# Values on half-width column tiles, shared key tiles and an earlier key projection in an attention mixer

## The chip, the cores and the metric

One core of a Trainium2 chip runs the whole program. The metric is device microseconds of that core, from the first to the last instruction of one launch; three runs of the kernel before are given, and one profiled run.

## What is computed

The program is a chain of blocks over 256 tokens of width 1024, in fp32: a gMLP mixer, a feed-forward part with a convolution, a differential attention, a second such feed-forward part, then a SwiGLU part, a mixer with two kinds of attention, another SwiGLU part and a last norm. The change touches only the mixer with two kinds of attention. In the reference it is (cut):

```python
u = rms_norm(x, mix_norm) @ w_in
c_q, c_kv, k_rope, mq, mk, mv = split(u)              # 384, 256, 32, 512, 512, 512 columns
q = rope_part(rms_norm(c_q, q_norm) @ w_uq)           # 8 heads of 64 + 32
k_nope, v = split(rms_norm(c_kv, kv_norm) @ w_ukv)    # 8 heads of 64 and 64
a_out = causal_softmax(q @ [k_nope, rope(k_rope)].T * 96 ** -0.5) @ v
b_out = causal_softmax(mq @ mk.T * 64 ** -0.5 - slope * distance) @ mv   # 8 heads of 64
x = x + concat(a_out, b_out) @ w_out
```

With 256 tokens the block-sparse attention (MoBA) has one block, its own, so it is dense and causal.

## The kernel before, in words

Weights come as 351 units of 128 x 1024 in fp32. A unit is loaded by SyncE (`Weights.load`, L296 on), its high part is copied by ScalarE (`prep_hi`, L305) and its low part is subtracted by VectorE (`prep_lo`, L311), and TensorE multiplies with both, so that three products in the fast fp32 format stand for one of full precision. `feed()` prepares a unit if fewer than `ahead` (6) prepared units are unused; a preparation also asks for loads up to `LOADS` (4) units on. Unit, high part and low part each take a place in one pool of 36 slots of 128 x 1024 (`slot`), and so do nearly all other large tiles: scores, their transposes, biases, values, compressed keys. A slot is handed to a new tile when the last reader of the tile before it is through; the engine that writes the new tile first waits for that reader.

The mixer stage runs from some 755 to 880 us. It works on pairs of heads: 16 heads are 8 pairs, which the table calls 0 to 7 (0 to 3 the first kind, 4 to 7 MoBA; q alone counts single heads). A pair has the two heads on the halves of the 128 partitions. The order of TensorE, ScalarE and VectorE is written out by hand in two tables, `MIX_BEFORE` (a scheduler may still move what is in it) and `MIX_PAIRS` (kept as written); each entry is a letter with its number:

- S: scores into PSUM on TensorE (L1148 for 0 to 3, all 128 rows of the array; L1152 for 4 to 7, two products of 64 rows side by side). N: `biased`, scale, bias and maximum on VectorE into the SBUF tile `s` (L846). E: exponentials on ScalarE (L1168). M: `normed`, division by the sum on VectorE (L1172, L1175).
- T: transposes of the probabilities on TensorE (L1182) and their copy on ScalarE (L1183). V: `values`, probabilities times values on TensorE (L1190). H and L: high and low part of the result (L1202, L1206). o: output projection (`part`, L535). b: the bias tile `al` (L1140).
- k: `mla_keys`, the rope-free keys `pkn` (L351 to L353; 4 column chunks). v: `mla_values` (L419). q: `mla_project`, queries of one head into `qs` (matmul `pqn`, copy L1129, VectorE L1130). p: `moba_project`, `mqk` of a pair of heads (matmul `pq` L375 to L378, ScalarE L390, VectorE L397).
- F, wh, wl: `feed`, high and low part of a weight unit; mid: loads the next gain.

Before S(4) the numbered steps 0 to 3 hold the projections q and p; from step 3 on a step is S(c), T(c−1), N(c), V(c−2), E, wl, M, H, L and then fillers.

The values stand in zero-padded tiles: for each half of the heads and each block of 128 tokens (tb) one tile of 128 x 4 x 2 x 128, in which the value columns of the first head of a pair are in the first 64 of 128 columns, and those of the second head in the last 64; GpSimd clears the rest (L1034), `put_values` (L1039) copies the other 64 columns with ScalarE. V then has 4 matmuls, all into the same 128 partitions of `po`, which add up. The compressed keys (`ckv`) are two tiles, high and low.

Where the mixer ends, a junction adds the result (L484), norms (L456, L445, L451, L501), transposes the tokens (L509) and splits them into `x` (L512 on ScalarE, L519 on VectorE); the last feed-forward part begins with token-major products `pz` (L419) on the units that are ready.

Of the kernel before, what the change touches and what calls it, by code (L numbers as in the profile page):

```python
# [11 lines left out]
F32R = mybir.dt.float32r  # L12
BF16 = mybir.dt.bfloat16
I32 = mybir.dt.int32
AF = mybir.ActivationFunctionType
# [5 lines left out]
P = 128  # L21
T = 256
# [9 lines left out]
AHEAD = 6  # L32
LOADS = 4
# [22 lines left out]
S, N_, E, M, T_, V, H_, L_, B_ = [(lambda c, x=x: (x, c, 0)) for x in "SNEMTVHLb"]  # L56
F, wh, wl, mid_ = ("F", 0, 0), ("wh", 0, 0), ("wl", 0, 0), ("mid", 0, 0)
k, v, q = (lambda c: ("k", c, 0)), (lambda tb: ("v", tb, 0)), (lambda h: ("q", h, 0))
p, o = (lambda c, n: ("p", c, n)), (lambda tb, c: ("o", tb, c))
MIX_BEFORE = [k(0), F, k(1), F, k(2), F, v(0), F, v(1), F, q(0), q(1), wh]  # L60


def _step(c, *fill):

    return [S(c), T_(c - 1), N_(c), V(c - 2), E(c), wl, M(c), H_(c - 2), L_(c - 2), *fill]


MIX_PAIRS = [
    S(0), N_(0), E(0), wl, q(2), M(0), wh, q(3), p(0, 1),
    S(1), T_(0), N_(1), E(1), wl, M(1), q(4), q(5), wh, k(3), p(1, 1),  # L70
    S(2), T_(1), N_(2), E(2), wl, M(2), q(6), q(7), V(0), H_(0), L_(0), wh,
    *_step(3, wh, p(2, 0), wl, B_(4), wh, o(0, 0)),
    *_step(4, mid_, wh, p(2, 1), wl, B_(5), wh, o(0, 1)),
    *_step(5, wh, p(3, 0), wl, B_(6), wh, o(0, 2)),
    *_step(6, wh, wl, B_(7), p(3, 1), wh),
    *_step(7, wh, o(0, 3), wl, wh, o(0, 4)), o(1, 0), wl, o(1, 1),
    T_(7), V(6), F, H_(6), L_(6), o(0, 5), V(7), H_(7), L_(7), o(0, 6), F, o(0, 7),
]
MIX = MIX_BEFORE + MIX_PAIRS

# [155 lines left out]
def _build(ctx, tc, nc, a, out):  # L236
# [10 lines left out]
    mm, act, vec = nc.tensor.matmul, nc.scalar.activation, nc.vector  # L247
# [3 lines left out]
    def nm(s):  # L251
        uid[0] += 1
        return f"{s}_{uid[0]}"

    def slot(name, dt=F32, shape=(P, D)):
        return slotp.tile(list(shape), dt, name=nm(name), tag="slot")
# [4 lines left out]
    def col(name, shape=(P, 1), dt=F32, bufs=4):  # L261
        return small.tile(list(shape), dt, name=nm(name), tag=name, bufs=bufs)

    def psm(name):
        return psM.tile([P, 512], F32, name=nm(name), tag="mm")
# [5 lines left out]
    def wide(tb, name):  # L271

        return [psA.tile([P, 512], F32, name=nm(name), tag=f"acc{tb}{q}") for q in range(2)]
# [13 lines left out]
    class Weights:  # L287
        def __init__(self):
            self.loaded, self.prepped, self.used, self.hi = [], [], 0, None
            self.ahead = AHEAD  # L290

        def load(self, n, cols=(slice(0, D),)):
            while len(self.loaded) < min(n, N_UNITS):
# [5 lines left out]

        def prep_hi(self, cols=(slice(0, D),)):  # L300
            n = len(self.prepped)
            self.load(n + LOADS)
            self.hi = slot(f"wh{n}", F32R)
            for c in cols:
                act(self.hi[:, c], self.loaded[n][:, c], AF.Copy)  # L305
# [37 lines left out]
    W = Weights()  # L343
    feed, unit = W.feed, W.unit
# [14 lines left out]
    def block(x, tb, n=KD):  # L359

        return [(x[:, k, 0, TB[tb]], x[:, k, 1, TB[tb]]) for k in range(n)]

    def pairs(x, tb, n):

        return [(x[0][:, tb, k, :], x[1][:, tb, k, :]) for k in range(n)]
# [661 lines left out]
    def mixer(x, late, tables, mid):  # L1027
        CS, dist, mask, kr, pair = tables
        cg = held["cg"]

        vals = [[slot("vals", shape=(P, 4, 2, P)) for tb in range(2)] for n in range(2)]
        for t in vals[0] + vals[1]:
            for n in range(2):
                nc.gpsimd.memset(t[:, :, n, (1 - n) * 64:(2 - n) * 64], 0.0)  # L1034

        def put_values(t, ps):
            ps = ps.rearrange("p (c n d) -> p c n d", c=4, n=2)
            for n in range(2):
                act(t[:, :, n, n * 64:(n + 1) * 64], ps[:, :, n, :], AF.Copy)  # L1039


        cq = [slot("cq", F32R, (P, 2, 3, P)) for n in range(2)]
        ckv = [slot("ckv", F32R, (P, 2, 2, P)) for n in range(2)]
        w1, w2 = W.lazy(8), W.lazy(2)
        stage = []

        def groups(tb):
            pa = wide(tb, "pmix")
            pk = psm("pckv")
            ops = token_major([(pa[0], 0, 512), (pa[1][:, :416], 512, 928)], block(x, tb), w1, D)  # L1050
            ops += token_major([(pk[:, :T], 0, T)], block(x, tb), w2, T)

            def done():
                cn = slot("cn", shape=(P, 768))

                kr_, two = pa[1][:, 384:416], cn[:, 640:768].rearrange("p (r s d) -> p r s d", r=2, s=2)
                for s_, d, n, o in ((0, 0, 32, 0), (1, 0, 16, 16), (1, 16, 16, 0)):
                    vec.tensor_copy(two[:, :, s_, d:d + n], kr_[:, o:o + n].unsqueeze(1).to_broadcast([P, 2, n]))
                for ps, n, o in ((pa[1][:, :384], 384, 0), (pk[:, :T], 256, 384)):
                    ms = col("cms")  # L1060
                    act(cn[:, o:o + n], ps, AF.Square, accum_out=ms)
                    r = rsqrt_col(ms, mul=1.0 / n)
                    vec.scalar_tensor_tensor(out=cn[:, o:o + n], in0=ps, scalar=r, in1=cg[:, o:o + n], op0=ALU.mult, op1=ALU.mult)
                put_values(vals[1][tb], pa[0])
                stage.append(cn)
            return ops, done
        start(x, late, groups)
# [47 lines left out]
        def mla_values(tb):  # L1115
            pvv = psm("pv")
            for f, _ in token_major([(pvv, 0, 512)], pairs(ckv, tb, 2), lambda i: kv(1), 512):
                f()
            put_values(vals[0][tb], pvv)

        wq = W.lazy(3)

# [62 lines left out]
        def values(g):  # L1185

            po, aT = psm("po")[:, :T], HH[g]["aT"]
            for n in range(2):
                for tb in range(2):
                    mm(out=po[:, tb * P:T], lhsT=vals[g // 4][tb][:, g % 4, n, :], rhs=aT[:, n, tb * T:tb * T + T - tb * P], start=(n + tb == 0), stop=(n + tb == 2))  # L1190
            HH[g] = {"po": po, "hid": hid_tiles()}

        hids, ws = [], {}
# [10 lines left out]
        def low(g):  # L1204
            hid = HH[g]["hid"]
            vec.tensor_sub(hid[1], HH[g]["po"], hid[0].bitcast(F32))  # L1206
            hids.append(hid)

        do = {
            "S": scores, "N": biased, "E": exps, "M": normed, "T": attend, "V": values, "H": high, "L": low, "b": bias,  # L1210
            "k": mla_keys, "v": mla_values, "q": mla_project, "p": moba_project, "o": project_out,
            "F": feed, "wh": W.prep_hi, "wl": W.prep_lo, "mid": mid,
        }

        def run(todo):

            for kind, i, c in todo:
                do[kind](*((i, c) if kind in ("p", "o") else () if kind in ("F", "wh", "wl", "mid") else (i,)))

        run(MIX_BEFORE)  # L1220
        with tc.manual_schedule(engines={mybir.EngineType.PE, mybir.EngineType.Activation, mybir.EngineType.DVE}):
            run(MIX_PAIRS)
        n = proj.count[1]
        assert proj.count[0] == 8 and all(o(1, c) in MIX for c in range(n))
        proj.held = [(hids[c], ws[c]) for c in range(n, 8)]
# [160 lines left out]
    for n, (c0, c1) in enumerate(ranges):  # L1386
        c, sum_ = slice(c0, c1), n < 2
# [16 lines left out]
    for c0, c1 in ranges[1:]:  # L1404
        c = slice(c0, c1)
# [47 lines left out]
```

## Time and profile before

| | |
|---|---|
| three runs | 1073.36, 1075.0, 1074.91 us, median 1074.91 |
| profiled execution | 1075.8 us, span of the trace 1074.0 |
| mean granted clock of TensorE | 0.996 |
| TensorE busy | 1054.1 us, 98% of the span |
| VectorE, ScalarE, GpSimd busy | 776.6, 656.7, 34.8 us |
| read from memory | 194.94 MB |

The table is from the first lines of the profile page. Busy time counts an engine's instructions from start to end; matmuls overlap, so what a group of matmuls costs is best read from the start of its first to the start of what follows it. Times in the trace are counted from the start of the span. An idle time in brackets names the instruction that ended it.

### The profile page before, as it was taken

Reading aid. Unit: us, or ns where it says so; the run is one execution under the profiler, and the core shown is the slowest. Engines: PE = TensorE matmul, PEld = TensorE weight load, DVE = VectorE, ACT = ScalarE, POOL = GpSimd, SP = SyncE. Lnnn points to the kernel's source line nnn. Section 1 sums busy time; section 2 is a strip of 40 time slices with the busy share of each in tenths; the row PEclk is TensorE's granted clock in tenths of the full one; section 3 lists DMA queues with packets and bytes.
Section 4 is the critical chain, followed back from the end, with each engine's and each line's share of the span. In section 5 each row is a group of like instructions: output and inputs, shape, how many; then the busy total and the mean of one; then the engine's idle time right before and its main releaser. Section 6 shows DMA issues by size and latency. Waiting matters only on the chain. (4 is left out here: it accounts for less than half of the span.)

```text
span 1074.0 us, 15781 instructions
## 1 busy us (share of the span) xinstructions
PE 1054.1 (98%) x5802; PEld 901.1 (84%) x5802; DVE 776.6 (72%) x1360; ACT 656.7 (61%) x1226; POOL 34.8 (3%) x65
## 2 busy tenths in 40 slices
PE   8999999999999999999999999999998999999997
PEld 6988888888787788888888888888897788888886
DVE  5896989887668768998776796665576857956633
ACT  5655867765478758776654675554476647755522
POOL 0100000000000110000000010000100000000000
PEclk9999999999999999999999999999999999999999
DMA  9946548652555456676525666553443455765501
GB/s 339 342 155 235 177 164 309 200 182 92 201 175 174 138 178 201 215 249 197 181 101 186 212 215 223 189 188 114 147 148 140 140 173 198 243 207 194 178 2 39
DMA packets 57246, 197.04 MB, mean 183 GB/s; under 512 B 6952, under 2 KB 9040, under 8 KB 57168
## 3 DMA queue, kind: packets, MB, share of 16 engines
q1 hardware_dynamic: 57024, 195.77, 54.4%
q8 instruction: 45, 0.74, 0.3%
q14 instruction: 33, 0.27, 0.1%
q10 hardware_dynamic: 144, 0.26, 0.1%
HBM read 194.94 MB, written 1.06 MB: 182 GB/s over the span
## 5 line engine op out<-in xcount | busy, mean ns | idle before, releaser
L311 DVE TENSOR_TENSOR wl<-w,wh 128x1024 fp32r<-128x1024 f32 (+1 forms) x352 | 424.8, 1219 | 130.8 <-ACT wh L305 91.2
L376 PE MATMUL pu<-x,wh 128*128 128x512 f32 x1216 | 427.2, 396 | 0.0
L305 ACT ACTIVATE wh<-w 128x1024 fp32r<-128x1024 f32 (+1 forms) x352 | 363.0, 1051 | 98.0 <-DVE wl L311 63.2
L375 PE MATMUL pu<-x,wl 128*128 128x256 f32 x1064 | 296.7, 279 | 0.0
L376 PEld LDWEIGHTS pu<-x,wh 128*128 128x128 f32 x1216 | 222.7, 188 | 44.6 <-DVE y L673 0.6
L375 PEld LDWEIGHTS pu<-x,wl 128*128 128x128 f32 x1064 | 200.6, 189 | 6.6
L535 PE MATMUL acc<-wh,hh 128*128 128x512 f32 x434 | 146.2, 397 | 1.3 <-DVE o L929 0.9
L535 PE MATMUL acc<-wl,hh 128*128 128x512 f32 x434 | 143.1, 390 | 0.0
L535 PE MATMUL acc<-wh,hl 128*128 128x512 f32 x434 | 142.1, 390 | 0.0
L390 ACT ACTIVATE low<-pu 128x256 f32<-128x256 f32 x152 | 57.4, 377 | 76.5 <-PE pu L376 75.8
L535 PEld LDWEIGHTS acc<-wh,hl 128*128 128x128 f32 x434 | 81.5, 188 | 17.5 <-DVE hl L429 0.3
L535 PEld LDWEIGHTS acc<-wl,hh 128*128 128x128 f32 x434 | 81.4, 188 | 16.9
L535 PEld LDWEIGHTS acc<-wh,hh 128*128 128x128 f32 x434 | 80.2, 188 | 15.5 <-ACT hh L428 1.4
L376 PE MATMUL pq<-x,wh 128*128 128x512 f32 x192 | 70.7, 405 | 0.0
L397 DVE TENSOR_TENSOR low<-pu,low 128x256 f32<-128x256 f32 x114 | 47.7, 418 | 17.3 <-ACT low L390 17.3
L419 PE MATMUL pz<-wh,x 128*128 128x256 f32 (+1 forms) x288 | 58.2, 323 | 0.8 <-DVE x L519 0.8
L428 ACT ACTIVATE hh<-y 128x256 fp32r<-128x256 f32 x88 | 35.6, 409 | 29.2 <-DVE y L673 15.1
L661 ACT ACTIVATE y<-low,cw 128x256 f32<-128x256 f32 x76 | 45.0, 592 | 11.7 <-DVE low L397 11.4
L419 PEld LDWEIGHTS pz<-wh,x 128*128 128x128 f32 x288 | 43.1, 189 | 6.5 <-DVE x L519 2.1
L375 PE MATMUL pq<-x,wl 128*128 128x256 f32 x168 | 47.6, 284 | 0.0
L456 ACT ACTIVATE junk<-h 128x512 bf16<-128x512 f32 (+1 forms) x32 | 19.9, 622 | 40.1 <-DVE h L484 19.1
L429 DVE TENSOR_TENSOR hl<-y,hh 128x256 fp32r<-128x256 f32 x88 | 36.6, 420 | 9.9 <-ACT hh L428 9.8
(235 smaller groups left out, 1257.0 us busy)
## 6 DMA issues: line engine op xcount, KB each, us to landing
w<-in_wall SPq DMA_DIRECT2D x349, 512.0 KB, 4.1
gain<-in_norm_g SPq DMA_DIRECT2D x7, 512.0 KB, 7.7
h<-in_x SPq DMA_DIRECT2D x4, 256.0 KB, 5.9
w<-in_wall SPq DMA_DIRECT2D x4, 256.0 KB, 5.2
bias<-fd SPq DMA_DIRECT2D x2, 512.0 KB, 10.2
gain<-in_ffn_norm SPq DMA_DIRECT2D x2, 512.0 KB, 4.8
gain<-in_a_ln_g SPq DMA_DIRECT2D x1, 512.0 KB, 6.3
gain<-in_a_ln_b SPq DMA_DIRECT2D x1, 512.0 KB, 6.6
```

The lines of the kernel that those rows point to most:

```text
L305: act(self.hi[:, c], self.loaded[n][:, c], AF.Copy)
L311: vec.tensor_sub(wl[:, c], w[:, c], wh[:, c].bitcast(F32))
L375: mm(out=ps[:, T:], lhsT=wl, rhs=x[:, k, 0], start=False, stop=False)
L376: mm(out=ps, lhsT=wh, rhs=x[:, k], start=(k == 0), stop=(k == KD - 1))
L390: act(low, ps[:, T:], AF.Copy)
L397: vec.tensor_add(out_, hi, low)
L419: mm(out=d, lhsT=x[lr], rhs=ws(u)[hl][:, c], start=(k == 0 and lr == 0 and hl == 0), stop=(k == last and lr == 1))
L428: act(hi, src, AF.Copy)
L429: vec.tensor_sub(lo, src, hi.bitcast(F32))
L456: act(junk[:, :src.shape[-1]], src, AF.Square, scale=1.0 / 32.0, accum_out=ms)
L535: mm(out=self.acc[tb][q], lhsT=hid[x][:, TB[tb]], rhs=w[hl][:, HALF[q]], start=s, stop=e)
L661: act(y, ps, AF.Identity, scale=cw[:, f, 2:3], bias=cw[:, f, 3:4])
```

## The change

- The values have two tiles without padding, of 128 x 2 x 512 (one for each half of the heads, both token blocks in it). The memsets are gone, and `put_values` is one copy of 128 x 512. V has 4 matmuls of 64 columns of weights: the two heads of a pair write partitions 0 to 63 and 64 to 127 of `po`, each with a sum of its own.
- The compressed keys, high and low, share one tile.
- k(3) moves from behind q(5) in step 1 into `MIX_BEFORE`; in step 0, q(3) goes ahead of a `wh`.
- In the mixer `loads` is 3 and `ahead` is 4; from `mid` on `ahead` is 6 again. One F of `MIX_BEFORE` is gone, and one pair of wh and wl of step 6.
- In step 7, T(6) and V(5) come ahead of S(7).

```diff
@@ -57,7 +57,7 @@
 F, wh, wl, mid_ = ("F", 0, 0), ("wh", 0, 0), ("wl", 0, 0), ("mid", 0, 0)
 k, v, q = (lambda c: ("k", c, 0)), (lambda tb: ("v", tb, 0)), (lambda h: ("q", h, 0))
 p, o = (lambda c, n: ("p", c, n)), (lambda tb, c: ("o", tb, c))
-MIX_BEFORE = [k(0), F, k(1), F, k(2), F, v(0), F, v(1), F, q(0), q(1), wh]
+MIX_BEFORE = [k(0), F, k(1), F, k(2), k(3), F, v(0), v(1), F, q(0), q(1), wh]
 
 
 def _step(c, *fill):
@@ -66,14 +66,14 @@
 
 
 MIX_PAIRS = [
-    S(0), N_(0), E(0), wl, q(2), M(0), wh, q(3), p(0, 1),
-    S(1), T_(0), N_(1), E(1), wl, M(1), q(4), q(5), wh, k(3), p(1, 1),
+    S(0), N_(0), E(0), wl, q(2), M(0), q(3), wh, p(0, 1),
+    S(1), T_(0), N_(1), E(1), wl, M(1), q(4), q(5), wh, p(1, 1),
     S(2), T_(1), N_(2), E(2), wl, M(2), q(6), q(7), V(0), H_(0), L_(0), wh,
     *_step(3, wh, p(2, 0), wl, B_(4), wh, o(0, 0)),
     *_step(4, mid_, wh, p(2, 1), wl, B_(5), wh, o(0, 1)),
     *_step(5, wh, p(3, 0), wl, B_(6), wh, o(0, 2)),
-    *_step(6, wh, wl, B_(7), p(3, 1), wh),
-    *_step(7, wh, o(0, 3), wl, wh, o(0, 4)), o(1, 0), wl, o(1, 1),
+    *_step(6, B_(7), p(3, 1), wh),
+    T_(6), V(5), S(7), N_(7), E(7), wl, M(7), H_(5), L_(5), wh, o(0, 3), wl, wh, o(0, 4), o(1, 0), wl, o(1, 1),
     T_(7), V(6), F, H_(6), L_(6), o(0, 5), V(7), H_(7), L_(7), o(0, 6), F, o(0, 7),
 ]
 MIX = MIX_BEFORE + MIX_PAIRS
@@ -287,7 +287,7 @@
     class Weights:
         def __init__(self):
             self.loaded, self.prepped, self.used, self.hi = [], [], 0, None
-            self.ahead = AHEAD
+            self.ahead, self.loads = AHEAD, LOADS
 
         def load(self, n, cols=(slice(0, D),)):
             while len(self.loaded) < min(n, N_UNITS):
@@ -299,7 +299,7 @@
 
         def prep_hi(self, cols=(slice(0, D),)):
             n = len(self.prepped)
-            self.load(n + LOADS)
+            self.load(n + self.loads)
             self.hi = slot(f"wh{n}", F32R)
             for c in cols:
                 act(self.hi[:, c], self.loaded[n][:, c], AF.Copy)
@@ -1028,19 +1028,12 @@
         CS, dist, mask, kr, pair = tables
         cg = held["cg"]
 
-        vals = [[slot("vals", shape=(P, 4, 2, P)) for tb in range(2)] for n in range(2)]
-        for t in vals[0] + vals[1]:
-            for n in range(2):
-                nc.gpsimd.memset(t[:, :, n, (1 - n) * 64:(2 - n) * 64], 0.0)
-
-        def put_values(t, ps):
-            ps = ps.rearrange("p (c n d) -> p c n d", c=4, n=2)
-            for n in range(2):
-                act(t[:, :, n, n * 64:(n + 1) * 64], ps[:, :, n, :], AF.Copy)
+        vals = [slot("vals", shape=(P, 2, 512)) for n in range(2)]
 
 
         cq = [slot("cq", F32R, (P, 2, 3, P)) for n in range(2)]
-        ckv = [slot("ckv", F32R, (P, 2, 2, P)) for n in range(2)]
+        kvt = slot("ckv", F32R, (P, 2, 2, 2, P))
+        ckv = [kvt[:, n] for n in range(2)]
         w1, w2 = W.lazy(8), W.lazy(2)
         stage = []
 
@@ -1061,7 +1054,7 @@
                     act(cn[:, o:o + n], ps, AF.Square, accum_out=ms)
                     r = rsqrt_col(ms, mul=1.0 / n)
                     vec.scalar_tensor_tensor(out=cn[:, o:o + n], in0=ps, scalar=r, in1=cg[:, o:o + n], op0=ALU.mult, op1=ALU.mult)
-                put_values(vals[1][tb], pa[0])
+                act(vals[1][:, tb, :], pa[0], AF.Copy)
                 stage.append(cn)
             return ops, done
         start(x, late, groups)
@@ -1116,7 +1109,7 @@
             pvv = psm("pv")
             for f, _ in token_major([(pvv, 0, 512)], pairs(ckv, tb, 2), lambda i: kv(1), 512):
                 f()
-            put_values(vals[0][tb], pvv)
+            act(vals[0][:, tb, :], pvv, AF.Copy)
 
         wq = W.lazy(3)
 
@@ -1185,9 +1178,10 @@
         def values(g):
 
             po, aT = psm("po")[:, :T], HH[g]["aT"]
-            for n in range(2):
-                for tb in range(2):
-                    mm(out=po[:, tb * P:T], lhsT=vals[g // 4][tb][:, g % 4, n, :], rhs=aT[:, n, tb * T:tb * T + T - tb * P], start=(n + tb == 0), stop=(n + tb == 2))
+            for tb in range(2):
+                for n in range(2):
+                    d = (2 * (g % 4) + n) * 64
+                    mm(out=po[n * 64:(n + 1) * 64, tb * P:T], lhsT=vals[g // 4][:, tb, d:d + 64], rhs=aT[:, n, tb * T:tb * T + T - tb * P], start=(tb == 0), stop=(tb == 1))
             HH[g] = {"po": po, "hid": hid_tiles()}
 
         hids, ws = [], {}
@@ -1206,10 +1200,14 @@
             vec.tensor_sub(hid[1], HH[g]["po"], hid[0].bitcast(F32))
             hids.append(hid)
 
+        def half_way():
+            W.ahead = AHEAD
+            mid()
+
         do = {
             "S": scores, "N": biased, "E": exps, "M": normed, "T": attend, "V": values, "H": high, "L": low, "b": bias,
             "k": mla_keys, "v": mla_values, "q": mla_project, "p": moba_project, "o": project_out,
-            "F": feed, "wh": W.prep_hi, "wl": W.prep_lo, "mid": mid,
+            "F": feed, "wh": W.prep_hi, "wl": W.prep_lo, "mid": half_way,
         }
 
         def run(todo):
@@ -1217,9 +1215,11 @@
             for kind, i, c in todo:
                 do[kind](*((i, c) if kind in ("p", "o") else () if kind in ("F", "wh", "wl", "mid") else (i,)))
 
+        W.loads, W.ahead = 3, 4
         run(MIX_BEFORE)
         with tc.manual_schedule(engines={mybir.EngineType.PE, mybir.EngineType.Activation, mybir.EngineType.DVE}):
             run(MIX_PAIRS)
+        W.loads, W.ahead = LOADS, AHEAD
         n = proj.count[1]
         assert proj.count[0] == 8 and all(o(1, c) in MIX for c in range(n))
         proj.held = [(hids[c], ws[c]) for c in range(n, 8)]
```

Three places in the order of instructions. First, TensorE in step 1 (`pkn` is k(3), `pqn` is q(5), `pq` is p(1, 1)); before:

```order
L353 MATMUL pqn_8554<-cq_7980,wl_1816_8292 128x256
L351 MATMUL pkn_8570<-ckv_7982,wh_1775_8079 128x256
L352 MATMUL pkn_8570<-ckv_7983,wh_1775_8079 128x256
L353 MATMUL pkn_8570<-ckv_7982,wl_1776_8081 128x256
L351 MATMUL pkn_8570<-ckv_7982,wh_1775_8079 128x256
L352 MATMUL pkn_8570<-ckv_7983,wh_1775_8079 128x256
L353 MATMUL pkn_8570<-ckv_7982,wl_1776_8081 128x256
L376 MATMUL pq_8579<-x_7883,wh_1829_8357 128x512
```

and now, behind the compressed keys' turn and ahead of the values (`pkn_8351` is the end of k(2), `pkn_8360` k(3), `pv` the values):

```order
L353 MATMUL pkn_8351<-ckv_7972,wl_1773_8070 128x256
L351 MATMUL pkn_8360<-ckv_7972,wh_1772_8068 128x256
L352 MATMUL pkn_8360<-ckv_7972,wh_1772_8068 128x256
L353 MATMUL pkn_8360<-ckv_7972,wl_1773_8070 128x256
L351 MATMUL pkn_8360<-ckv_7972,wh_1772_8068 128x256
L352 MATMUL pkn_8360<-ckv_7972,wh_1772_8068 128x256
L353 MATMUL pkn_8360<-ckv_7972,wl_1773_8070 128x256
L419 MATMUL pv_8369<-wh_1775_8076,ckv_7972 128x512
```

k(3) stands between k(2) and v(0), one step earlier, and both halves of the compressed keys have one name.

Second, TensorE around S(7) (`pq` is the end of p(3, 1), `s` S(7), `pT` T(6), `po` V(5), `acc` the output projection); before:

```order
L376 MATMUL pq_8980<-x_7883,wh_1909_8748 128x512
L1152 MATMUL s_9004<-mqk_8250,mqk_8249 128x128
L1152 MATMUL s_9005<-mqk_8250,mqk_8249 128x128
L1152 MATMUL s_9004<-mqk_8250,mqk_8249 128x256
L1152 MATMUL s_9005<-mqk_8250,mqk_8249 128x256
L1182 MATMUL pT_9011<-ident,s_8943 128x128 x3
L1182 MATMUL pT_9016<-ident,s_8943 128x128 x3
L1190 MATMUL po_9027<-aT_8932,vals_7970 128x256
L1190 MATMUL po_9027<-aT_8932,vals_7971 128x128
L1190 MATMUL po_9027<-aT_8932,vals_7970 128x256
L1190 MATMUL po_9027<-aT_8932,vals_7971 128x128
L535 MATMUL acc_8344<-wh_1925_8805,hh_8870 128x512
```

and now:

```order
L376 MATMUL pq_8945<-x_7883,wh_1921_8805 128x512
L1175 MATMUL pT_8970<-ident,s_8914 128x128 x3
L1175 MATMUL pT_8975<-ident,s_8914 128x128 x3
L1184 MATMUL po_8980<-aT_8903,vals_7969 64x256 x2
L1184 MATMUL po_8980<-aT_8903,vals_7969 64x128 x2
L1145 MATMUL s_8987<-mqk_8237,mqk_8236 128x128
L1145 MATMUL s_8988<-mqk_8237,mqk_8236 128x128
L1145 MATMUL s_8987<-mqk_8237,mqk_8236 128x256
L1145 MATMUL s_8988<-mqk_8237,mqk_8236 128x256
L535 MATMUL acc_8331<-wh_1936_8860,hh_8841 128x512
```

T(6) and V(5) stand ahead of S(7), and the matmuls of V have 64 columns of weights.

Third, the start of the last feed-forward part, where `pt` are the transposes of the second token block, `x` its copy and `pz` the first products. ScalarE before:

```order
L456 ACTIVATE junk_9209,ms_9143<-h_82 128x512
L305 ACTIVATE wh_2025_9247<-w_1987_9049 128x1024
L305 ACTIVATE wh_2028_9259<-w_1990_9061 128x1024
L305 ACTIVATE wh_2033_9288<-w_2004_9128 128x1024
L512 ACTIVATE x_9141<-pt_9270 128x4x128
L305 ACTIVATE wh_2036_9297<-w_2024_9245 128x1024
L512 ACTIVATE x_9141<-pt_9271 128x4x128
```

and now:

```order
L456 ACTIVATE junk_9180,ms_9114<-h_82 128x512
L512 ACTIVATE x_9112<-pt_9255 128x4x128
L305 ACTIVATE wh_2016_9208<-w_1988_9070 128x1024
L512 ACTIVATE x_9112<-pt_9256 128x4x128
L305 ACTIVATE wh_2019_9221<-w_1994_9099 128x1024
L305 ACTIVATE wh_2022_9232<-w_2014_9204 128x1024
L305 ACTIVATE wh_2025_9244<-w_2015_9206 128x1024
```

TensorE now, at the end of the twelve products on the two units that are ready (`wh_1989`, `wh_1995` and their low parts):

```order
L419 MATMUL pz_9192<-wl_1990_9074,x_9112 128x256
L419 MATMUL pz_9192<-wh_1995_9101,x_9112 128x256
L419 MATMUL pz_9192<-wl_1996_9103,x_9112 128x256
L509 MATMUL pt_9255<-ident,xn_9188 128x128 x4
L509 MATMUL pt_9256<-ident,xn_9188 128x128 x4
L419 MATMUL pz_9326<-wh_1989_9072,x_9112 128x512
L419 MATMUL pz_9192<-wh_2016_9208,x_9112 128x256
```

ScalarE copies the first half of `x` ahead of any weight unit instead of behind three, and TensorE goes straight from the products on two units to the eight transposes; before, the products on two more units stood between.

## Rows read from the trace of the kernel before

**Rows 1.** The page, busy time of each engine and share of the span.

```profile
PE 1054.1 (98%) x5802; PEld 901.1 (84%) x5802; DVE 776.6 (72%) x1360; ACT 656.7 (61%) x1226; POOL 34.8 (3%) x65
```

**Rows 2.** Waits, 755 to 900 us: us in total, times, longest.

```profile
PE s L1148 <- DVE qs L1130: 3.1, 4, 1.1
...
PE s L1152 <- DVE mqk L397: 2.2, 1, 2.2
...
PEld s L1152 <- issue: 1.1, 3, 0.4
...
PE pz L419 <- DVE wl L311: 0.4, 1, 0.4
```

**Rows 3.** Timeline of VectorE, step 1: start, duration, operation [idle before].

```profile
809.84 0.42 DVE L397 TENSOR_TENSOR mqk<-pq,low 128x256 f32<-128x256 f32 x1
814.27 0.29 DVE L846 CUSTOM_DVE_ANT_0 s<-s,tab 128x128 f32<-128x128 f32 x1 [4.01 <-PE pkn L352]
...
817.77 0.88 DVE L1130 TENSOR_TENSOR qs<-pqn,trig 64x256 f32<-64x256 f32 x2
```

**Rows 4.** Timeline of PE, steps 0 to 3.

```profile
801.55 1.62 PE L1148 MATMUL s<-ks,qs 128*128 128x128 f32 x8 [0.22 <-DVE qs L1130]
...
813.47 0.28 PE L351 MATMUL pkn<-ckv,wh 128*128 128x256 f32 x1
...
814.19 0.40 PE L376 MATMUL pq<-x,wh 128*128 128x512 f32 x1
...
818.25 1.58 PE L1148 MATMUL s<-ks,qs 128*128 128x128 f32 x8 [1.08 <-DVE qs L1130]
...
824.63 1.58 PE L1148 MATMUL s<-ks,qs 128*128 128x128 f32 x8 [0.68 <-DVE qs L1130]
826.04 0.82 PE L1182 MATMUL pT<-ident,s 128*128 128x128 f32 x6
```

**Rows 5.** Timeline of PE, steps 6 and 7.

```profile
846.62 0.93 PE L1152 MATMUL s<-mqk,mqk 64*128 64x128 f32 x8
847.47 0.88 PE L1182 MATMUL pT<-ident,s 128*128 128x128 f32 x6
848.18 1.47 PE L1190 MATMUL po<-aT,vals 128*128 128x256 f32 x8
849.41 0.48 PE L376 MATMUL pq<-x,wh 128*128 128x512 f32 x1
...
854.72 1.65 PE L1152 MATMUL s<-mqk,mqk 64*128 64x128 f32 x8 [2.23 <-DVE mqk L397]
856.30 1.54 PE L1182 MATMUL pT<-ident,s 128*128 128x128 f32 x6
857.63 1.62 PE L1190 MATMUL po<-aT,vals 128*128 128x256 f32 x8
859.01 0.71 PE L535 MATMUL acc<-wh,hh 128*128 128x512 f32 x2
```

**Rows 6.** S(5) to S(6): busy PE, PEld, DVE, ACT, POOL; granted clock.

```profile
839.44:846.62 7.18, 7.18 (x46) 5.84 (x45) 6.27 (x20) 5.17 (x15) 0.00 (x0) 1.00 0.40 146
```

**Rows 7.** Timeline of VectorE, step 6.

```profile
852.17 1.22 DVE L311 TENSOR_TENSOR wl<-w,wh 128x1024 fp32r<-128x1024 f32 x1
```

**Rows 8.** Two windows, the same columns as rows 6.

```profile
805.00:810.00 5.00, 3.88 (x24) 3.13 (x22) 2.18 (x8) 3.20 (x10) 0.00 (x0) 1.00 0.29 105
...
855.00:860.00 5.00, 5.00 (x26) 4.09 (x26) 2.34 (x9) 2.61 (x10) 0.00 (x0) 0.71 0.61 188
```

**Rows 9.** Timelines of PE, then VectorE, start of the last feed-forward part.

```profile
883.73 0.52 PE L419 MATMUL pz<-wh,x 128*128 128x512 f32 x2
...
886.45 0.50 PE L419 MATMUL pz<-wl,x 128*128 128x256 f32 x2 [0.36 <-DVE wl L311]
...
883.84 1.42 DVE L501 SCALAR_TENSOR_TENSOR xn<-h,rs_r,gain 128x512 f32<-128x512 f32 x2 [0.73 <-POOL rs_r L451]
```

**Rows 10.** Timeline of GpSimd, start of the mixer stage.

```profile
784.50 0.56 POOL L451 TENSOR_TENSOR rs_r<-rs_e,pw 128x1 f32<-128x1 f32 x1 [19.98 <-DVE rs_e L443]
```

## The prediction

> **What bounds the kernel now.** First the page: TensorE (PE) is busy for 98% of the span [rows 1]. A part that takes nothing off PE's own work, or off a wait of PE, is worth nothing, so I look for those alone. Second, the table of waits in the last mixer stage, which is the only stage that the diff touches: PE waits there 3.1 us in four pieces for the query tiles `qs`, 2.2 us in one piece for the MoBA query tile `mqk`, and 0.4 us at the start of the last feed-forward part [rows 2]. Third, the timelines of VectorE (DVE) and PE around each of these, to see what the late producer itself stood behind.
>
> DVE reaches `biased(1)` at about 810.2 and then stands for 4.01 us until PE has run a `pkn` matmul [rows 3]. `biased(1)` does not read `pkn`. What it needs is a place for its own tile `s`, and the slot that it is given holds the second half of the compressed keys, whose last reader is k(3). PE runs k(3) only at 813.47 [rows 4]: the wait is one for a buffer. Behind it on DVE stand the normalising of pair 1 and the products for `qs` of heads 4 and 5, which end at 818.65 [rows 3]; S(2) waits 1.08 us for the first of them and starts at 818.25 [rows 4].
>
> **The change part by part.**
>
> *A, k(3) early.* The same six matmuls run either way; by their starts k(3) takes 814.19 − 813.47 = 0.72 us [rows 4], so the move itself is neutral. With k(3) long done and the two compressed-key tiles in one, `biased(1)` finds a slot and DVE starts it at about 810.3 instead of 814.27. Then `qs` of head 5 is there before PE has finished p(1, 1), and S(2) follows p(1, 1) without its 1.08 us. The wait before S(1) goes too: its `qs` (head 3) is now copied ahead of a weight unit on ScalarE, not behind it. It is the longest of the four, 1.1 us [rows 2]. Together 2.2, and perhaps 0.1 of the 0.22 before S(0) [rows 4]: I take **2.3**, which puts S(2) at about 815.95 against 818.25. From S(2) to S(3) the chain through DVE (S, biased, exponentials, normalise, `qs`) sets the pace and not PE: 824.63 − 818.25 = 6.38 us [rows 4], which stays. So S(3) keeps the 2.3 us and no more, and what V(0) saves only lengthens the wait before S(3). Bounds: 0 (another slot holds DVE as long) and 3.1 (all `qs` waits gone).
>
> *B, the values product on half-width weights.* A pair's V now takes 849.41 − 848.18 = 1.23 us [rows 5]. After the change the same columns stream, but two 64-column products stand on two column positions. No row shows such a product. The nearest is the MoBA score, which has two 64-row products side by side: 847.47 − 846.62 = 0.85 us [rows 5], against 826.04 − 824.63 = 1.41 us for the full-array score with the same columns [rows 4], a ratio of 0.60. I take 0.83 for V, close to that row, and so 0.40 us for each of the seven pairs 1 to 7: **2.8**. PE is the bound where these stand, as long as DVE keeps up: DVE is busy for 6.27 us of the 7.18 us of a step [rows 6], which would become 6.78. Bounds: 0.62 us a pair (exact halving) to 1.38 us (one after the other, plus the 0.15 us by which the MoBA score's 0.85 misses half of 1.41). The sum then moves by +1.5 or −3.9.
>
> *C, step 7.* Before S(7) PE idles 2.23 us for `mqk` [rows 5]. DVE has a weight unit's low part (1.22 us) ahead of it [rows 7], and the granted clock then reads 0.71 in the next five microseconds [rows 8]. In rows: S, T and V take 1.58, 1.33 and 1.38 us there, against 0.85, 0.71 and 1.23 one step earlier [rows 5]. That is 1.5 us on top of the 2.23. The change removes that weight unit from step 6 and puts T(6), V(5) ahead of S(7), where they cover what is left of `mqk`'s lateness. Both costs go: **3.8**, of which 0.1 may remain as a short wait. Bounds: 2.2 (only the wait goes) and 3.8. Next in line is T(7), which waits for pair 7's softmax: four parts of the output projection still stand between S(7) and T(7), and I count them as cover enough.
>
> *D, start of the last feed-forward part.* Two weight units fewer are ready there. Before, PE runs twelve rows on units 285 and 286 up to 883.73, then rows on units 287 and 288 up to the transposes of the second token block, and waits only 0.36 us [rows 9]. In the order of the changed kernel those transposes follow the twelve rows at once. They need `xn`, whose first half ends at 884.55 (half of the 1.42 us from 883.84) [rows 9]: 0.8 us, some 1.1 with the signals between engines; 0.3 more for the second half; then ScalarE and DVE must make `x` before the next product may start, 0.75, and 0.1 for the weight unit behind it. About 2.2 us idle instead of 0.36: a loss of **1.85**. Bounds: 0.9 to 3.4 (with a clock fall, below).
>
> *At nothing.* Eight memsets leave GpSimd, whose next work comes after 19.98 us of idleness [rows 10]. ScalarE's two copies for the values become one of the same columns, with the attention a long way off. Weights that are loaded three ahead rather than four have more than a unit's work to land in. If that cover were gone, a late unit would cost PE a wait of a weight preparation, about 1.2 us [rows 7].
>
> **Sum**: 2.3 + 2.8 + 3.8 − 1.85 = 7.05, say 7.1. The profiled execution took 1075.8 us by its own time, 0.9 over the median of the three runs (1074.91); so 1068.7 for it, and **1067.8** on the median. A measurement of this kernel can tell about 0.2%, 2.15 us, from no change.
>
> The MoBA score's ratio of 0.60 is the only row on which 0.83 rests. The Trainium skill, TensorEngine Tiling (Array Packing), section Theoretical Speedup, gives up to 2x where a dimension is 64 or less, by which V would be 0.62 and the sum 8.55 where the row makes it 7.05. The same page's section Key Properties speaks against the change: a switch of the tiling mode drains TensorE. The rows on the MoBA score agree with something between the two.
>
> **The rivals.**
> 1. *The two column tiles overlap in full*: V is 1.23 / 2 = 0.62 us, and 7 × 0.21 = 1.5 more: 1066.3. For it: the two products of a pair read their own weights and write their own partitions, so nothing orders them. Against it: so do the two of the MoBA score, and they stayed at 0.60 [rows 4, 5]. Chance 0.12. This is the case that the Trainium skill, TensorEngine Tiling (Array Packing), section Theoretical Speedup, gives as the most.
> 2. *The clock falls at D.* PE idled 2.23 us before S(7), and the window behind it shows 0.71; it idled about 1.1 us in the window 805 to 810, which reads 1.00 [rows 8]. D's idle time is 2.2 us, but in pieces with transposes between them. If the clock falls, it costs what it cost at step 7, 1.5 us: 1069.3. Chance 0.23.
> 3. *The column tiles run one after the other*: 1.38 us each, the sum loses 2.8 and 7 × 0.15: 1067.8 + 3.9 = 1071.7. For it: both tiles take their moving data from the same 128 rows, while the MoBA tiles have rows of their own, so the nearest row may not carry over. Chance 0.14.
> 4. *The change does not free DVE*: the slot given to `biased(1)`'s tile is held by some other late reader, and A is 0: 1067.8 + 2.3 = 1070.1. For it: one slot pool serves everything, and fewer tiles shift every assignment. Against it: k(3) was the only late reader in the waits. Chance 0.07.
> 5. *Slower: PE drains at each change of column position.* The only price near it is the wait on issue of the MoBA score's weight loads, 1.1 us in three, 0.37 each [rows 2]. Four changes a pair make V 4 × 0.37 = 1.48 us longer than 1.23: 7 × 1.48 = 10.4, and 0.8 of V(0), beyond the 0.68 before S(3) [rows 4] that would hide the rest, against 2.3 + 3.8 − 1.85 = 4.25: 6.95 slower than 1074.91, 1081.9. It decides from V = 1.23 + 4.25 / 7 = 1.84 us on, 0.15 for each change. Against it: the MoBA scores change position too and are fast. Chance 0.05.
>
> **How the numbers follow.** The forecast keeps 0.39. Cases 1 to 4 are all faster than 1072.76 (0.2% under the median), except case 3 together with a clock fall (1073.2, no difference). Faster 0.90, same 0.05, slower 0.05. The range goes from 1065.5 (case 1, with the 0.8 that A has up to its upper end) to 1072.1 (case 3 and a little): it leaves out case 5, case 3 with the clock fall, and the errors of several terms in one direction.
>
> **What would show it.** Right: no wait of DVE on `pkn`; S(2) 2.3 us earlier; a V near 0.83 from its first row to the next matmul's; no wait of over 0.3 us before S(7), and clock 1.00 there; at the start of the last feed-forward part PE waiting about 2 us, for `xn` and `x`. Wrong: V above 1.2, a new wait in steps 1 to 7 for a weight unit (the three loads ahead), a T(7) that waits for its softmax, or a slow stretch after the idle time at D.

## The result, and the profile after

The changed kernel takes 1068.32 us, median of 4 runs (1066.73 to 1069.14), against 1074.13 us for the kernel before in the same comparison: ratio 0.9945, interval 0.993 to 0.996. In a second comparison with 5 runs it took 1068.37 us, ratio 0.9938 (0.9924 to 0.9952). The forecast was 1067.8 us.

The page of the changed kernel (its profiled execution took 1066.73 us by its own time, span 1064.9) shows 5.5 us less of busy TensorE than [rows 1]:

```profile
PE 1048.6 (98%) x5802; PEld 893.3 (84%) x5802; DVE 776.7 (73%) x1360; ACT 656.4 (62%) x1222; POOL 32.5 (3%) x57
```

To see where the time went, I cut both traces at two matmuls that every version has: `pkt`, ahead of the first keys, and the first `pz` of the last feed-forward part. In the timeline of TensorE before:

```profile
793.69 0.59 PE L1101 MATMUL pkt<-kr,pair 128*128 128x256 f32 x2
...
881.50 0.50 PE L419 MATMUL pz<-wh,x 128*128 128x512 f32 x1 [0.28 <-DVE x L519]
```

and after, with the transposes of the first token block (868.71) and the rows behind the first `pz`:

```profile
791.66 0.59 PE L1094 MATMUL pkt<-kr,pair 128*128 128x256 f32 x2
...
868.71 1.03 PE L509 MATMUL pt<-ident,xn 128*128 128x128 f32 x8
...
870.72 0.51 PE L419 MATMUL pz<-wh,x 128*128 128x512 f32 x1 [0.28 <-DVE x L519]
...
872.58 0.28 PE L419 MATMUL pz<-wl,x 128*128 128x256 f32 x1
873.86 1.32 PE L509 MATMUL pt<-ident,xn 128*128 128x128 f32 x8 [1.01 <-DVE xn L501]
875.92 0.86 PE L419 MATMUL pz<-wh,x 128*128 128x512 f32 x3 [0.75 <-DVE x L519]
```

From `pkt` to the first `pz` ("mixer stage" below) the kernel before takes 881.50 − 793.69 = 87.81 us, the changed one 870.72 − 791.66 = 79.06: 8.75 us won. From the first `pz` to the end ("end part") it is 1074.0 − 881.50 = 192.50 against 1064.9 − 870.72 = 194.18: 1.68 us lost. The sum is 7.07 us; the forecast's sum was 7.05. The rest of the difference of the two spans, 2.03 us, lies ahead of `pkt`. There PE's work is the same, and 1.97 of it is there within the first 14 us, where both traces have the same four matmuls (timelines of TensorE, before and then after):

```profile
13.36 1.09 PE L1261 MATMUL accv<-wl,x 128*128 128x512 f32 x4
...
11.39 1.09 PE L1261 MATMUL accv<-wl,x 128*128 128x512 f32 x4
```

Profiles of one program differ as much: `fed` below has the changed kernel's code up to there and reaches `pkt` at 793.80. So it is no effect of the change.

Term by term. VectorE no longer stands before `biased(1)` [rows 3]: its first instruction follows the one ahead of it at once (timeline of VectorE after).

```profile
807.28 0.42 DVE L397 TENSOR_TENSOR mqk<-pq,low 128x256 f32<-128x256 f32 x1
807.62 0.28 DVE L846 CUSTOM_DVE_ANT_0 s<-s,tab 128x128 f32<-128x128 f32 x1
```

S(2) starts 813.69 − 791.66 = 22.03 us behind `pkt`, against 24.56 before, S(3) 28.25 against 30.94 (timeline of PE after, where S(3) now has the wait of 1.14 us that the forecast told of):

```profile
813.69 1.47 PE L1141 MATMUL s<-ks,qs 128*128 128x128 f32 x8
...
819.91 1.58 PE L1141 MATMUL s<-ks,qs 128*128 128x128 f32 x8 [1.14 <-DVE qs L1123]
821.32 0.82 PE L1175 MATMUL pT<-ident,s 128*128 128x128 f32 x6
822.07 0.87 PE L1184 MATMUL po<-aT,vals 128*64 128x256 f32 x8
822.87 0.50 PE L376 MATMUL pq<-x,wh 128*128 128x512 f32 x1
```

V(1) takes 822.87 − 822.07 = 0.80 us, where V took 1.23 [rows 5]. Around step 7 (timeline of PE after) no wait is left before S(7), and T(6), V(5) and S(7) take 0.75, 0.89 and 0.85 us, where S, T and V took 1.58, 1.33 and 1.38 [rows 5]. In step 6 the transposes ahead of V are 0.80 us long from start to start, 0.09 more than in [rows 5]:

```profile
840.98 0.93 PE L1145 MATMUL s<-mqk,mqk 64*128 64x128 f32 x8
841.84 0.87 PE L1175 MATMUL pT<-ident,s 128*128 128x128 f32 x6
842.64 0.87 PE L1184 MATMUL po<-aT,vals 128*64 128x256 f32 x8
843.44 0.50 PE L376 MATMUL pq<-x,wh 128*128 128x512 f32 x1
...
846.37 0.82 PE L1175 MATMUL pT<-ident,s 128*128 128x128 f32 x6
847.12 0.87 PE L1184 MATMUL po<-aT,vals 128*64 128x256 f32 x8
848.01 0.93 PE L1145 MATMUL s<-mqk,mqk 64*128 64x128 f32 x8
848.86 0.74 PE L535 MATMUL acc<-wh,hh 128*128 128x512 f32 x2
```

The waits of PE in the mixer stage and behind it that answer to [rows 2] (us in total, times, longest):

```profile
PE s L1141 <- DVE qs L1123: 1.1, 1, 1.1
...
PE pz L419 <- DVE x L519: 1.0, 2, 0.7
...
PE pt L509 <- DVE xn L501: 1.0, 1, 1.0
```

The wait before S(7) is gone, one of the four for `qs` is left, and two new ones stand at the start of the end part: for `xn`, and then for `x`.

### The profile page after: what moved, and what is told of

It reads as the page before. It is cut to its first block, busy times and chain, and to the rows that moved or that the text cites. A ratio compares the mean times of both kernels' runs of the same rounds, so it can differ in the third digit from the quotient of the medians.

```text
span 1064.9 us, 15760 instructions
## 1 busy us (share of the span) xinstructions
PE 1048.6 (98%) x5802; PEld 893.3 (84%) x5802; DVE 776.7 (73%) x1360; ACT 656.4 (62%) x1222; POOL 32.5 (3%) x57
```

## The experiments

Each kernel was timed against the kernel before in several rounds and profiled once. "Mixer stage" and "end part" are from its trace, cut as above; they repeat from trace to trace within some 0.1 us where nothing is changed, far better than the whole time does.

| kernel | ratio to before, interval | mixer stage | end part |
|---|---|---|---|
| before | | 87.81 | 192.50 |
| changed | 0.9945 (0.993 to 0.996) | 79.06 | 194.18 |
| changed, again | 0.9938 (0.9924 to 0.9952) | 79.09 | 195.84 |
| v_alone | 0.9991 (0.9983 to 1.0) | 86.04 | 192.48 |
| k_early | 0.9982 (0.9973 to 0.9991) | 85.39 | 192.46 |
| step7_alone | 0.9976 (0.9965 to 0.9987) | 84.08 | 192.39 |
| padded_values | 0.9968 (0.9958 to 0.9978) | 81.36 | 194.17 |
| step7_old_order | 0.9963 (0.9949 to 0.9977) | 80.65 | 195.79 |
| deep_feed | 0.9933 (0.9921 to 0.9945) | 79.48 | 192.50 |
| fed | 0.9928 (0.9915 to 0.9942) | 79.07 | 192.53 |
| fed_qs_first | 0.9918 (0.9906 to 0.993) | 78.12 | 192.50 |

**k_early**: term A alone, both of its moves (k(3), and q(3) ahead of a `wh`).

```diff
-MIX_BEFORE = [..., k(2), F, v(0), F, v(1), F, q(0), q(1), wh]
+MIX_BEFORE = [..., k(2), k(3), F, v(0), F, v(1), F, q(0), q(1), wh]
-    ..., M(0), wh, q(3), p(0, 1), ... q(4), q(5), wh, k(3), p(1, 1),
+    ..., M(0), q(3), wh, p(0, 1), ... q(4), q(5), wh, p(1, 1),
```

> The kernel before with k(3) ahead of the values and q(3) ahead of a weight unit, nothing else. Theory (term A is the wait for the compressed keys' slot): VectorE's wait of 4.0 us on pkn is gone, S(2) and S(3) start 2.3 to 2.7 us earlier, and the run is 2.3 to 2.7 us shorter, ratio about 0.9977; the wait before S(7) stays at 2.2 us. Rival 1 (the slot that biased(1) gets is held by another reader): VectorE still stands 2 us or more there and the ratio is 1.000. Rival 2 (a later wait takes the time back): S(3) comes 2.5 us earlier, but the wait before S(7) grows by as much.

The mixer stage is 2.42 us shorter, and the table of waits has no wait of VectorE for `pkn` any more; before S(7) PE waits as long as before:

```profile
PE s L1152 <- DVE mqk L397: 2.2, 1, 2.2
...
PE s L1148 <- DVE qs L1130: 1.0, 2, 0.7
```

So the wait was one for k(3), the compressed keys' last reader, and it did not move to another slot. Both rivals are out. The two key tiles in one slot were not needed for it.

The 2.42 us belong to both moves together, and no run has one of them alone. The wait of 1.11 us inside S(1) is one for `qs` of head 3. In the kernel before, ScalarE copies that head behind a `wh`, which had itself waited 1.54 us for PE (timeline of ScalarE, then of PE, before):

```profile
807.94 1.06 ACT L305 ACTIVATE wh<-w 128x1024 fp32r<-128x1024 f32 x1 [1.54 <-PE pq L375]
...
809.90 0.92 PE L1148 MATMUL s<-ks,qs 128*128 128x128 f32 x4 [1.11 <-DVE qs L1130]
```

In k_early the copy for head 3 no longer stands behind that `wh`, and PE waits neither in S(1) nor before S(2); of the waits for `qs` those before S(0) (0.30) and S(3) (0.68) are left.

**v_alone**: term B alone, out of the old padded tiles.

```diff
-            for n in range(2):
-                for tb in range(2):
-                    mm(out=po[:, tb * P:T], lhsT=vals[g // 4][tb][:, g % 4, n, :], ...)
+            for tb in range(2):
+                for n in range(2):
+                    mm(out=po[n * 64:(n + 1) * 64, tb * P:T], lhsT=vals[g // 4][tb][:, g % 4, n, n * 64:(n + 1) * 64], ...)
```

> The kernel before with one edit: the values product uses 64-column halves of the same zero-padded tiles, on two column positions. Theory (term B is PE time per pair and adds up with the others): each V takes about 0.80 us instead of 1.23, of which 0.09 goes back into the transposes ahead of it, so 0.34 for each of the pairs 1 to 7, 2.4 us in all: ratio about 0.9978. Rival (term B is only worth what the waits leave): VectorE, not PE, sets when S(7) may start, so that what V(1) to V(4) save only lengthens the wait before S(7), from 2.23 us to about 3.3, and 1 us or less is left in all: ratio 0.999 or above.

Between the two: 1.77 us by the trace, more than the rival's 1 us and less than the theory's 2.4. By the whole time it is 1.0 us (0 to 1.8), which is the rival's figure; but the wait did not grow to the 3.3 us that the rival wanted. S(7) comes only 0.91 us earlier behind `pkt` (60.12 against 61.03) although four V ran ahead of it, because its wait grew from 2.23 to 2.61 us (timeline of PE):

```profile
852.40 0.93 PE L1152 MATMUL s<-mqk,mqk 64*128 64x128 f32 x8 [2.61 <-DVE mqk L397]
853.26 1.33 PE L1182 MATMUL pT<-ident,s 128*128 128x128 f32 x6
854.52 1.55 PE L1190 MATMUL po<-aT,vals 128*64 128x256 f32 x8
856.00 1.15 PE L535 MATMUL acc<-wh,hh 128*128 128x512 f32 x2
```

VectorE is late with `mqk` there, so a faster PE waits longer. The other 0.86 us come behind S(7), where three V are left; at 0.34 each they would give 1.02. The lower clock is there in both profiles, at V(5) too: 856.00 − 854.52 = 1.48 us here, 1.38 before [rows 5].

**padded_values**: the changed kernel without term B.

```diff
-        vals = [slot("vals", shape=(P, 2, 512)) for n in range(2)]
+        vals = [[slot("vals", shape=(P, 4, 2, P)) for tb in range(2)] for n in range(2)]
...
```

Memsets, `put_values` and the full-width products come back with it, as in the kernel before.

> The changed kernel with the values back in four zero-padded tiles and full-width products. Theory (behind the new step 7 nothing eats what V saves): V 1.23 us again and 0.34 us a pair lost for the pairs 1 to 7, 2.4 us, and V(0) nothing: mixer stage about 81.5 us against 79.06. In the kernel before the same edit was worth 1.77 us, so the new step 7 adds 0.6. Rival (two slots fewer cost a wait too): 82 us or more, with a wait for a slot in the trace.

81.36 − 79.06 = 2.30 us, and no wait for a slot. V is 1.23 us again, and the transposes ahead of it 0.71 (timeline of PE, T(5) and V(4)):

```profile
843.26 0.87 PE L1183 MATMUL pT<-ident,s 128*128 128x128 f32 x6
843.97 1.47 PE L1191 MATMUL po<-aT,vals 128*128 128x256 f32 x8
845.20 0.48 PE L376 MATMUL pq<-x,wh 128*128 128x512 f32 x1
```

In the changed kernel the same two take 0.80 each (841.84, 842.64 and 843.44 in the timeline above): V saves 0.43, the transposes give back 0.09. The Trainium skill, TensorEngine Tiling (Array Packing), section Key Properties, says that a change of the tiling mode drains TensorE. The 0.09 us between full-array transposes and column tiles agrees with it. That they are this drain and nothing else about the column tiles, no run shows.

**step7_alone**: term C alone.

```diff
-    *_step(6, wh, wl, B_(7), p(3, 1), wh),
-    *_step(7, wh, o(0, 3), wl, wh, o(0, 4)), o(1, 0), wl, o(1, 1),
+    *_step(6, B_(7), p(3, 1), wh),
+    T_(6), V(5), S(7), N_(7), E(7), wl, M(7), H_(5), L_(5), wh, o(0, 3), wl, wh, o(0, 4), o(1, 0), wl, o(1, 1),
```

> The kernel before with step 7 in the new order and one weight unit fewer in step 6, nothing else; as many units are ready at the start of the last feed-forward part as before. Theory (term C is a wait of 2.2 us and 1.5 us of PE at the lower clock behind it): no wait before S(7) above 0.5 us, granted clock 1.00 in the five microseconds behind it, 3.8 us shorter, ratio about 0.9965. Rival (the lower clock in the one profile of the kernel before is not there in every run): only the wait counts, 2.2 us, ratio about 0.998.

3.73 us by the trace, no wait before S(7), and the granted clock, the third figure from the end, is 1.00 in both windows (timeline of PE, then the windows):

```profile
851.39 0.82 PE L1182 MATMUL pT<-ident,s 128*128 128x128 f32 x6
852.04 1.47 PE L1190 MATMUL po<-aT,vals 128*128 128x256 f32 x8
853.45 0.93 PE L1152 MATMUL s<-mqk,mqk 64*128 64x128 f32 x8
```

```profile
850.00:855.00 5.00, 5.00 (x34) 4.15 (x33) 3.19 (x13) 2.30 (x6) 0.00 (x0) 1.00 0.60 211
855.00:860.00 5.00, 5.00 (x25) 4.07 (x24) 4.96 (x15) 3.83 (x11) 0.00 (x0) 1.00 0.61 203
```

By the whole time it is 2.9 us at the median and 3.8 at the end of the interval. That fits the rival in part: the profile of the kernel before is one in which the lower clock was there, but 6 of the 46 runs of the kernel before that were timed beside these versions have a mean granted clock of 1.000 (1072.45 to 1073.01 us). A fall that costs 1.5 us of 1074 would leave no more than 0.999, so in them the clock did not fall.

**step7_old_order**: the changed kernel with S(7) ahead of T(6) and V(5) again.

```diff
-    T_(6), V(5), S(7), N_(7), E(7), wl, M(7), ...
+    S(7), T_(6), N_(7), V(5), E(7), wl, M(7), ...
```

> The changed kernel with S(7) back ahead of T(6) and V(5); the weight unit stays out of step 6. Theory (the unit's absence takes 1.2 us off the 2.2 us wait, the new order covers the rest): PE waits about 1.0 us before S(7), the clock stays 1.00 behind so short a wait, mixer stage 80.0 to 80.3 us against 79.06. Rival 1 (VectorE's low part was the whole cause, the order covers nothing): no wait over 0.3 us, 79.1 us. Rival 2 (the wait is shorter but the clock falls all the same): 81.5 us or more.

80.65 us, between the theory and the second rival, and PE waits 1.48 us:

```profile
850.70 0.93 PE L1145 MATMUL s<-mqk,mqk 64*128 64x128 f32 x8 [1.48 <-DVE mqk L397]
```

The kernel nearest to this with the unit still there is v_alone, where V is as short as here: its wait is 2.61 us. So the missing unit takes about 1.13 us, near the 1.22 of its low part on VectorE [rows 7], as the theory had it, and the new order the other 1.48. The theory's wait was 1.0 us because it started from the 2.23 of the kernel before. Behind 1.48 us of idleness the clock did not fall: it reads 1.00 from 850 to 880. It fell later in this run (0.66, third from the end), and the end part is 195.79 us, 1.6 more than in the changed kernel's trace:

```profile
880.00:885.00 5.00, 4.77 (x21) 4.25 (x22) 4.75 (x6) 5.00 (x7) 0.00 (x0) 0.66 0.28 99
```

**change_again**: the changed kernel once more, because of that.

> The changed kernel itself once more, with a profile and the granted clock of every run. Theory (the clock falls behind D's idle time in some executions, as in the profile of the old order of step 7: 195.79 us from the first pz on instead of 194.18): the runs come in two groups some 1.5 to 2 us apart, those of the upper group with a mean clock 0.001 to 0.002 lower, and the profile shows either 194.2 us with clock 1.00 or 195.8 us with a window near 0.7. Rival (the spread of the runs is that of the first weights' arrival alone): no such tie between time and clock, and the end of the program 194.2 us.

This time the end part of the changed kernel itself takes 195.84 us. The windows (granted clock third from the end) show the clock falling behind the waits for `xn` and `x`, 0.75 and 0.91:

```profile
870.00:875.00 5.00, 3.83 (x24) 2.96 (x22) 2.81 (x6) 1.81 (x4) 0.55 (x1) 1.00 0.81 269
875.00:880.00 5.00, 4.14 (x18) 3.35 (x19) 4.03 (x6) 4.21 (x6) 0.00 (x0) 0.75 0.45 168
880.00:885.00 5.00, 5.00 (x31) 4.54 (x30) 5.00 (x6) 5.00 (x6) 0.00 (x0) 0.91 0.26 94
```

where the first profile of the same program has 1.00:

```profile
870.00:875.00 5.00, 3.71 (x22) 2.59 (x21) 3.48 (x6) 1.60 (x4) 0.55 (x1) 1.00 0.67 256
875.00:880.00 5.00, 4.25 (x28) 3.81 (x27) 4.56 (x5) 5.00 (x7) 0.00 (x0) 1.00 0.33 108
```

So the second rival of the prediction, the clock that falls at D, happens in some executions of the changed kernel and not in others; it costs 195.84 − 194.18 = 1.66 us. The times of the runs don't settle how often: with a mean clock of 0.999 they are 1067.54, 1067.6 and 1068.96 us, with 0.997 1068.37 and 1069.53. The four runs of the first comparison lie the same way, 1066.73 and 1067.6 with 0.999, 1069.04 and 1069.14 with 0.997. But the mean covers the whole run, and so does not say where the clock fell.

**fed**: the changed kernel with the two units back.

```diff
-    T_(7), V(6), F, H_(6), L_(6), o(0, 5), V(7), H_(7), L_(7), o(0, 6), F, o(0, 7),
+    T_(7), V(6), F, H_(6), L_(6), o(0, 5), F, V(7), H_(7), L_(7), o(0, 6), F, o(0, 7), F,
```

> The changed kernel with two more feeds behind o(0, 5) and o(0, 7), so that four weight units instead of two are ready at the start of the last feed-forward part. Theory (term D is the lack of these two units): PE's waits there, 1.0 us for xn and 0.75 us for x, fall to the 0.4 us of the kernel before, and the run is 1.7 us shorter than the changed kernel, 7.5 to 8.8 us shorter than the kernel before: ratio 0.992 to 0.993. Rival (the two units only move the work: their preparation on ScalarE and VectorE delays the output's parts and the norm): PE waits as long before the junction instead, ratio 0.9945 as for the changed kernel.

The end part is 192.53 us, as in the kernel before, and the mixer stage pays nothing for it. The two waits are gone. A short one for a weight unit has come (0.3 for `wh`); the 0.3 for `x` is the wait before the first `pz`, which the traces of the kernel before and of the changed kernel have too:

```profile
PE pz L419 <- ACT wh L305: 0.3, 1, 0.3
PE pz L419 <- DVE x L519: 0.3, 1, 0.3
```

1066.68 us at the median. Term D is shown: it is the lack of the two units, 1.65 us in this trace.

**deep_feed**: the changed kernel without the lower depth.

```diff
-        W.loads, W.ahead = 3, 4
```

> The changed kernel with four loads and six prepared units ahead in the mixer, as before. Theory (the lower depth is only there to spare slots, and the slots that the values and keys gave back would carry the old depth): four units ready at the start of the last feed-forward part, the end of the program from the first pz on 192.5 us instead of 194.18, mixer stage 79.1 us: 1.7 us shorter than the changed kernel, ratio to the kernel before about 0.993. Rival (with the old depth a tile of steps 0 to 7 gets a slot that is read late, as biased(1) did before): a new wait of 0.5 us or more on VectorE or ScalarE for a slot, mixer stage 79.6 us or more, and no gain over the changed kernel.

The end part is 192.50 us, so D goes this way too. No engine shows a wait for a slot, so the slots would have carried the old depth; but the mixer stage is 0.42 us longer. Two more units are prepared ahead of S(0), and VectorE, itself waiting for ScalarE's high part, makes `qs` behind one of them (timeline of VectorE):

```profile
800.61 1.22 DVE L311 TENSOR_TENSOR wl<-w,wh 128x1024 fp32r<-128x1024 f32 x1 [2.08 <-ACT wh L305]
801.86 0.88 DVE L1123 TENSOR_TENSOR qs<-pqn,trig 64x256 f32<-64x256 f32 x2
```

S(0) starts 8.93 us behind `pkt` instead of 8.21. In all it is 1.3 us better than the changed kernel by the trace (79.48 + 192.50 against 79.06 + 194.18).

**fed_qs_first**: fed, and one exchange in step 2 against the wait that term A left before S(3).

```diff
-    S(2), T_(1), N_(2), E(2), wl, M(2), q(6), q(7), V(0), ...
+    S(2), T_(1), N_(2), E(2), wl, q(6), q(7), M(2), V(0), ...
```

> The kernel with the two feeds (fed), and in step 2 q(6) and q(7) ahead of M(2), so that VectorE makes qs of heads 6 and 7 before it normalises pair 2. Theory (S(3) waits 1.1 us only because its qs stand behind M(2) on VectorE): S(3) starts 0.5 to 0.9 us earlier and T(2) still finds its probabilities in time; mixer stage from pkt to the first pz 78.2 to 78.6 us against 79.07, ratio to the kernel before 0.992. Rival (the wait moves to T(2), whose probabilities come 0.9 us later): S(3) earlier, T(2) waits, no gain: 79.1 us.

S(3) waits 0.15 us, T(2) follows it without one (timeline of PE), and the mixer stage is 78.12 us, 0.95 less than in `fed` and a little under the range that was expected:

```profile
819.73 0.87 PE L1184 MATMUL po<-aT,vals 128*64 128x256 f32 x8
820.75 1.58 PE L1141 MATMUL s<-ks,qs 128*128 128x128 f32 x8 [0.15 <-DVE qs L1123]
822.16 0.82 PE L1175 MATMUL pT<-ident,s 128*128 128x128 f32 x6
```

1065.05 us, the fastest version: 0.9918 of the kernel before, 3.3 us under the changed kernel by the medians, 2.6 by the traces (78.12 + 192.50 against 79.06 + 194.18).

## Why the prediction was right, point by point

- **A** (2.3): 2.42 alone. The reason holds, a slot whose last reader is k(3). In the changed kernel S(3) is 2.69 us earlier; the chain from S(2) to S(3) held to within 0.16 us (6.22 against 6.38), and S(3)'s wait is the 1.14 us left.
- **B** (2.8): the nearest row was a good one, 0.80 us for V where 0.83 was forecast. What the step missed is the 0.09 us by which the transposes are longer ahead of column tiles: 7 × 0.34 = 2.4 instead of 2.8, and 2.30 measured (padded_values). That column tiles run one after the other, and that they overlap in full, are both out for this product: 0.80 / 1.23 = 0.65. The slower rival, a drain at each change of position, which needed a V of 1.84 us, is out as well. The Trainium skill's up to 2x (TensorEngine Tiling (Array Packing), section Theoretical Speedup) is not reached here.
- **C** (3.8): 3.73 by the trace, which is also what the forecast's own rows add up to (2.23 + 1.50); it took 0.07 more. The forecast took the lower clock from the one profile of before as a cost of every run; step7_alone's 2.9 us by the median, and the runs of before whose clock is 1.000 throughout, say that this is too much for the median run.
- **D** (−1.85): −1.68 in one trace, −3.34 in the other, where the clock fell. The forecast's pieces had no rows for the 0.3 of signals, the 0.3 of the second half and the 0.75 for `x`. The trace shows 1.01 us ahead of the transposes, 1.32 − 1.03 = 0.29 more within the eight of them than in the first block's, and 0.75 ahead of the products, 2.05 in all against the forecast's 2.2; its 0.1 for the weight unit behind has no row of its own. For the fall of the clock, the forecast had a rival with 0.23. It is no either-or: the same program does both.
- **The sum**: the parts alone give 2.42 + 1.77 + 3.73 = 7.92 in the mixer stage, together they give 8.75. Half a microsecond of the difference is V's, which S(7)'s wait ate when it stood alone (2.30 against 1.77). The other 0.3 fits the lower depth, which none of the three has and which is worth 0.42 us in the mixer stage (deep_feed). By the two traces the net is 7.07 us, within 0.02 of the forecast, and that is luck: B and D were each too large, with opposite signs, the 0.42 was not in the sum, and the trace of before has the lower clock at S(7) where that of the changed kernel has none at D. With change_again's trace the net is 5.38; by the medians it is 5.8 and 6.2, whose intervals (4.3 to 7.5, and 5.2 to 8.2 us) hold 7.07. The time itself, 1068.32 against 1067.8, came closer than the net because the median of the kernel before was 0.8 us lower in this comparison than the 1074.91 that the forecast started from. That the medians are lower fits a clock that falls in some runs of the changed kernel and is not there in all of the kernel before; the 6 of 46 runs above show the second for some runs, but the share of each was not measured.
- **At nothing**: no wait for a slot or a load appeared, and GpSimd's and ScalarE's edits left no trace on PE. The lower depth did not come out at nothing, though: it gave the 0.42 us in the mixer stage and it cost D, so that it lost 1.3 us in all (deep_feed).

## What to carry to other kernels

When an engine waits for an operation whose result it does not read, look for the slot that its output was given, and move the slot's last reader forward. A saving ahead of a wait that another engine ends is partly eaten by it, so remove that wait first or count the two together. Weight units that are ready at a stage's start are cover for the norm and transposes there: whoever thins out the feeding must see who filled that gap.

## What the runs showed of the hardware

- Where PE idled 2.23, 2.61 and 2.24 us in one piece before S(7) (before, v_alone, k_early), the granted clock fell to its lower level of 1.2 GHz in all three profiles: in windows of half a microsecond it reads 0.50 from 855.0 to 857.5 (before), 854.0 to 856.5 (v_alone) and 851.5 to 854.5 (k_early), and 1.00 again within a microsecond; behind 1.48 us in one piece it did not (one profile); behind 1.0 and 0.75 us with transposes between, it fell in two of four profiles (of changed, change_again, padded_values and step7_old_order, in the second and the last; 0.50 from 877.5 to 880.5 in change_again). One profile of a clock at such a place is one throw.
- The runs of one version spread by 1.2 us (deep_feed, 5 runs) to 4.4 us (padded_values, 10 runs). Part of it lies in the first microseconds: the second group of transposes starts between 8.72 us (changed) and 10.28 us (before) in the eleven profiles, in most of them behind a wait for the input's loads. The granted clock differs there too: from 5 to 10 and 10 to 15 us it reads 0.80 and 0.86 in the profile of before, below 1.00 also in deep_feed, fed and fed_qs_first, and 1.00 in the other seven. It is not the whole cause, as step7_old_order with 1.00 reaches `pkt` last, at 794.36. The two segments of the table are free of that, and so were the better measure here.
